# Low parts of projection weights kept in DRAM, with other load orders, in a hybrid decoder layer

## The chip, the cores and the metric

The kernel runs on one core of a Trainium2 chip. The metric is the device time of one execution in microseconds, as the median of several runs. The engines are TensorE (PE, matrix products; its weight loads are shown as PEld), VectorE (DVE), ScalarE (ACT), GpSimd (POOL) and SyncE (SP). SP computes nothing here: it issues loads, in program order (its queue is shown as SPq). POOL issues stores and a few loads.

## The reference

One layer on 2048 tokens of width 1024, in float32. A conditioning vector gives shift, scale and gate vectors (the ada part). The layer is a mixer and an MLP, each behind an RMS norm:

```python
def hybrid_mixer(h, w_in, ..., w_out):
    proj = h @ w_in                       # 1024 -> 4608 and a few columns
    z, xbc, dt_raw, glu_a, glu_b = jnp.split(proj, ...)
    xbc = silu(causal_dwconv(xbc, conv_ssd_w, conv_ssd_b))
    y = ssd_chunked(xh, dt, a, bm, cm) + d_skip * xh
    y = gated_rmsnorm(y, z, ssd_norm_w)
    u = glu_a * sigmoid(glu_b)
    u = causal_dwconv(u, conv_cf_w, conv_cf_b)          # 31 taps
    u = silu(layernorm(u, cf_ln_w, cf_ln_b))
    return concatenate([y, u]) @ w_out    # 2048 -> 1024
# x = x + gate1 * mixer(...);  x = x + gate2 * (relu(h @ w1) ** 2 @ w2);  final RMS norm
```

## The kernel before

**Precision.** Each float32 operand of a large product is split into a high part (a copy rounded to the TensorE format fp32r) and a low part (the rest). A product of two split operands is three matmuls: high by high, high by low, low by high. A weight block is a tile of 128 x 1024 elements, 512 KB. `split_w` loads it on SP, ACT writes the high part and DVE the low part:

```python
raw = t_wr()
nc.sync.dma_start(raw, src)
hi, lo = dst or (t_turn("wh", 2, [P, D], F32R), t_turn("wl", 2, [P, D], F32R))
A.activation(hi, raw, AF.Copy)
V.tensor_tensor(lo, raw, f(hi), SUB)
```

The raw tiles rotate through three buffers (wr0 to wr2), the high and low parts through two each (wh, wl). So the parts of block n+2 can be written only when TensorE has read those of block n.

**Stages.** The tokens are cut into two halves and four quarters of 512 tokens. Times in the profile of before, from the span's start: ada and norm to about 55 us; in_proj, convolutions and SSD of half 0 (36 weight blocks of `w_in`) to about 500, and of half 1 (the same 36 blocks again) to 1009; the mix of half 0, which is out_proj with two quarters of 16 blocks of `w_out` (`mix_q`, L854 to L856), to 1190; up of half 0 to 1500 and its down to 1880; the mix of half 1 (quarters 2 and 3) to 2047; up of half 1 to 2375; its down to 2680; the final norm. Every weight block of `w_in` is thus split twice, and every one of `w_out` four times.

**Up and down.** Up forms its products in a Strassen-like scheme of seven products per block pair (`w1_prep`, products at L1003 to L1005). For each pair mp, DVE makes sums s and u of the weights (L985 to L987, in tiles tp0 and tp1), then ACT and DVE split the seven operands (L885, L886). The raw weights x and y of pair mp+1 come into wr0 to wr2. Down of half 0 is plain (`down_`, L1349 to L1351). Down of half 1 uses seven products too (`down7_of`): the operands that up made (`keep_ops`, stored to DRAM as op_d through POOL) are loaded again (`op_raw`) and split (`op_split`); its weights come through `w2_prep`. `ahead()` is the part of down that is issued beside the last steps of up: it is a generator, and up advances it a step at a time.

**Convolution and layer norm.** `conv_cf` runs at low priority beside other stages and stores its result v_d through POOL. `ln_cf` is the layer norm of that result, for pieces of 256 tokens: load v_d into cu0 and cu1, sum on DVE (L410 to L413), a product with ones on PE (L416, tile bm), squares, a second such product (L213, a part of `chan_rsqrt`), scale, store to m_d (L435). It is a generator; each call of `ln_step` advances it by one step. `ln_step(0)` is called in half 1's in_proj and in the mix of half 0; `ln_step(1)` in half 0's down, one call a weight block.

**What sets the order.** A scheduler of the Tile framework orders instructions by priority within each engine, with the program order as the base; `urgent()` raises a priority, `later()` lowers it. Each engine then runs its own list strictly in order, and so does each issuing queue: an instruction that waits holds up what stands behind it on the same engine.

Of the kernel before, what the change touches and what calls it, by code (L numbers as in the profile page):

```python
# [46 lines left out]
def tile_layer(ctx, tc, x, w_ada, w_mod, vecs, w_in, w_dt, w_out, w1, w2, w2p, out):  # L47
# [243 lines left out]
    def split_w(src, dst=None):  # L291
        raw = t_wr()
        nc.sync.dma_start(raw, src)
        hi, lo = dst or (t_turn("wh", 2, [P, D], F32R), t_turn("wl", 2, [P, D], F32R))
        with urgent():
            A.activation(hi, raw, AF.Copy)  # L296
            V.tensor_tensor(lo, raw, f(hi), SUB)  # L297
        return hi, lo

# [202 lines left out]
    for half in range(2):  # L502
        pre = {}
        if half == 0:
# [5 lines left out]
            for sg in range(4):  # L510
# [3 lines left out]
                held[W0[sg]] = split_w(w_in[W0[sg]], (d_bx(F32R), d_bx(F32R)))  # L514
# [54 lines left out]
            for n, b in enumerate(W1):  # L569
                held[b] = split_w(w_in[b])  # L570
# [9 lines left out]
        else:  # L580
            held = {b: split_w(w_in[b]) for b in W0[:2]}
# [68 lines left out]
        def proj(blk):  # L650
            whl = held[blk] if blk in pre else split_w(w_in[blk])
# [109 lines left out]
        for g in range(2):  # L761
# [44 lines left out]
            whl = split_w(w_in[g * 4 + 1])  # L806
# [9 lines left out]
            whl = [split_w(w_in[g * 4 + 2]), split_w(w_in[g * 4 + 3], (d_bx(F32R), d_bx(F32R)))]  # L816
# [19 lines left out]
    def mix_q(q, acts, x2, side, whl=None):  # L836
# [3 lines left out]
        ws = [w_out[m, pos if q % 2 else 1 - pos] for mg in (0, 4) for pos in range(2) for m in range(mg, mg + 4)]  # L840
        if whl is None:
            whl = split_w(ws[0])
        for mg in (0, 4):
            pss = {}
            for pos in range(2):
                for m in range(mg, mg + 4):
# [15 lines left out]
                    if n < 16:  # L862
                        whl = split_w(ws[n])
# [29 lines left out]
    def mix(half, m0):  # L893
# [25 lines left out]
        def side(n):  # L919
            tick()  # L920
            if half == 0:
                ln_step(0)
# [55 lines left out]
    def w1_prep(sums0):  # L978
        x, y = r2(t_raw(w1[0], "wr0")), r2(t_raw(w1[1], "wr1"))
        for mp in range(NU):  # L980
            src = dict(a11=x[:, 1, :], a22=x[:, 0, :], a12=y[:, 1, :])
            for n in range(2 if mp < NE else 0, 7):
                if n == 2:
                    s, u = (r2(t_at(t)) for t in (("tp0", "tp1") if mp else sums0))
# [89 lines left out]
    def up(half, hx, second, ahead):  # L1074
        early(half, hx, second)
        prep = w1_prep(plan[half][7])
# [147 lines left out]
    def down7_of():  # L1224
# [5 lines left out]

        def op_raw(kb, n):
            return [t_raw(op_d[kb][n][:, h * D : (h + 1) * D]) for h in range(2)]
# [4 lines left out]

        def ahead():
            ws.extend((next(prep), next(prep)))
            yield  # L1240
            raws = op_raw(0, 0)
            yield
            op_split(0, raws)
            ws.append(next(prep))
            raws = op_raw(0, 1)
            yield
            op_split(1, raws)
            raws = op_raw(0, 2)
            ws.append(next(prep))
            yield  # L1250
            op_split(2, raws)
            raws = op_raw(0, 3)
            yield
            op_split(3, raws)
            yield
# [4 lines left out]
        def down():  # L1260
            sqs, ends = [None] * 2, []

            for kb in range(4):
                for g in range(2):
                    b1, b2, b3 = [None] * 2, [None] * 2, [None] * 2
                    raws = None
                    for n in range(7):
                        if kb == 0 and g == 0 and 4 <= n:
                            op_split(n, op_raw(0, n))
# [3 lines left out]
                        for l in range(2):  # L1273
                            mp = 2 * g + l
                            if kb == 0 and n == 0:
# [210 lines left out]
```

## Time and profile before

| | |
|---|---|
| median of 3 runs | 2706.15 us (2704.84 to 2707.09) |
| the profiled execution's own time | 2701.98 us |
| its span | 2699.8 us |
| mean granted TensorE clock | 0.992 |
| PE busy | 2634.3 us, 98% |
| DVE busy | 2181.0 us, 81% |
| ACT busy | 1400.4 us, 52% |
| POOL busy | 300.2 us, 11% |
| moved by DMA | 407.82 MB, mean 151 GB/s |

A row of an engine gives its busy time. A wait is read from the idle time before an instruction and the event that ended it. Where TensorE's granted clock falls to half, a matmul of 512 columns takes 0.43 us from start to start in place of 0.23, and it counts as busy all that time, so idle time and clock are read separately. TensorE's busy time holds ends that are modelled.

### The profile page before, as it was taken

Reading aid. Unit: us, or ns where it says so; the run is one execution under the profiler, and the core shown is the slowest. Engines: PE = TensorE matmul, PEld = TensorE weight load, DVE = VectorE, ACT = ScalarE, POOL = GpSimd, SP = SyncE. Lnnn points to the kernel's source line nnn. Section 1 sums busy time; section 2 is a strip of 40 time slices with the busy share of each in tenths; the row PEclk is TensorE's granted clock in tenths of the full one; section 3 lists DMA queues with packets and bytes.
Section 4 is the critical chain, followed back from the end, with each engine's and each line's share of the span. In section 5 each row is a group of like instructions: output and inputs, shape, how many; then the busy total and the mean of one; then the engine's idle time right before and its main releaser. Section 6 shows DMA issues by size and latency. Waiting matters only on the chain. (4 is left out here: it accounts for less than half of the span.)

```text
span 2699.8 us, 34186 instructions
## 1 busy us (share of the span) xinstructions
PE 2634.3 (98%) x12460; PEld 2149.7 (80%) x12460; DVE 2181.0 (81%) x3368; ACT 1400.4 (52%) x2169; POOL 300.2 (11%) x469
## 2 busy tenths in 40 slices
PE   7999999999999999999999999999999999999997
PEld 4778888788788778888888888878888778778886
DVE  7889999998996668999999874466547776588886
ACT  5757546676754755546566312354336445554452
POOL 1320120030021000011011000000001222100000
PEclk9999999999999999999999999999999999999998
DMA  7463233232322356545434733355735554564541
GB/s 288 140 214 109 79 102 110 86 111 79 118 86 78 123 177 231 164 161 188 148 137 141 242 111 100 109 195 181 244 122 188 204 197 148 197 212 146 167 148 63
DMA packets 130921, 407.82 MB, mean 151 GB/s; under 512 B 15937, under 2 KB 24769, under 8 KB 130753
## 3 DMA queue, kind: packets, MB, share of 16 engines
q1 hardware_dynamic: 97728, 294.07, 32.7%
q0 software_dynamic: 33024, 111.57, 11.6%
q8 instruction: 98, 1.61, 0.2%
q14 instruction: 71, 0.57, 0.1%
HBM read 304.65 MB, written 100.93 MB: 150 GB/s over the span
## 5 line engine op out<-in xcount | busy, mean ns | idle before, releaser
L306 PE MATMUL mm<-big,wh 128*128 128x512 f32 x1024 | 411.3, 402 | 2.4 <-DVE tp L716 1.8
L308 PE MATMUL mm<-big,wl 128*128 128x512 f32 x1024 | 403.9, 394 | 0.0
L307 PE MATMUL mm<-big,wh 128*128 128x512 f32 x1024 | 400.3, 391 | 0.0
L296 ACT ACTIVATE wh<-wr 128x1024 fp32r<-128x1024 f32 x167 | 176.1, 1055 | 314.5 <-PE mm L855 114.0
L297 DVE TENSOR_TENSOR wl<-wr,wh 128x1024 fp32r<-128x1024 f32 x167 | 203.6, 1220 | 70.1 <-ACT wh L296 59.2
L306 PEld LDWEIGHTS mm<-big,wh 128*128 128x128 f32 x1024 | 192.3, 188 | 51.9 <-issue 9.2
L308 PEld LDWEIGHTS mm<-big,wl 128*128 128x128 f32 x1024 | 192.3, 188 | 43.6 <-issue 3.2
L307 PEld LDWEIGHTS mm<-big,wh 128*128 128x128 f32 x1024 | 192.4, 188 | 42.9 <-issue 4.7
L1003 PE MATMUL mm<-big,wh 128*128 128x512 f32 x536 | 212.3, 396 | 9.1 <-ACT wh L885 3.7
L1004 PE MATMUL mm<-big,wh 128*128 128x512 f32 x536 | 210.7, 393 | 0.0
L1005 PE MATMUL mm<-big,wl 128*128 128x512 f32 x532 | 207.2, 389 | 1.2 <-DVE wl L886 1.2
L856 PE MATMUL mm<-big,wl 128*128 128x512 f32 x512 | 200.1, 391 | 1.4 <-DVE wl L297 1.4
L854 PE MATMUL mm<-big,wh 128*128 128x512 f32 x512 | 200.0, 391 | 0.4 <-ACT wh L296 0.4
L855 PE MATMUL mm<-big,wh 128*128 128x512 f32 x512 | 199.3, 389 | 0.0
L1349 PE MATMUL mm<-big,wh 128*128 128x512 f32 x496 | 194.9, 393 | 0.0
L1351 PE MATMUL mm<-big,wl 128*128 128x512 f32 x496 | 194.0, 391 | 0.3 <-DVE wl L297 0.3
L1350 PE MATMUL mm<-big,wh 128*128 128x512 f32 x496 | 194.1, 391 | 0.0
L387 DVE SCALAR_TENSOR_TENSOR ca<-cu,const,ca 128x512 f32<-128x512 f32 x240 | 178.6, 744 | 1.5 <-ACT ca L381 1.2
L390 DVE SCALAR_TENSOR_TENSOR ca<-ca,const,ca 128x512 f32<-128x512 f32 x240 | 178.3, 743 | 0.0
L1005 PE MATMUL mm<-big,wh 128*128 128x512 f32 x440 | 173.3, 394 | 0.0
L1003 PE MATMUL mm<-big,wl 128*128 128x512 f32 x436 | 170.3, 391 | 1.5 <-ACT cc L1113 1.2
L389 DVE SCALAR_TENSOR_TENSOR ca<-cu,const,ca 128x513 f32<-128x513 f32 x224 | 167.2, 746 | 3.7 <-ACT ca L383 3.7
(346 smaller groups left out, 5919.4 us busy)
## 6 DMA issues: line engine op xcount, KB each, us to landing
wr<-in_w_dram SPq DMA_DIRECT2D x120, 512.0 KB, 3.5
wr<-in_w_in_dram SPq DMA_DIRECT2D x72, 512.0 KB, 3.4
wr<-in_w_out_dram SPq DMA_DIRECT2D x64, 512.0 KB, 4.1
wr<-op_d SPq DMA_DIRECT2D x56, 512.0 KB, 4.6
ca<-in_w_ada_dram POOLq DMA_DIRECT2D x64, 256.0 KB, 3.5
tp<-ac_d SPq DMA_DIRECT2D x32, 512.0 KB, 4.3
wr<-m_d SPq DMA_DIRECT2D x32, 512.0 KB, 4.2
op_d<-tt POOLq DMA_DIRECT2D x64, 256.0 KB, 2.6
```

Of the source, the lines that this page charges most:

```text
L297: V.tensor_tensor(lo, raw, f(hi), SUB)
L306: T.matmul(ps, lhsT=hi[:, c], rhs=a[:, 0, :], start=(k == 0), stop=False)
L307: T.matmul(ps, lhsT=hi[:, c], rhs=a[:, 1, :], start=False, stop=False)
L308: T.matmul(ps, lhsT=lo[:, c], rhs=a[:, 0, :], start=False, stop=(k == KT - 1))
L854: T.matmul(ps, lhsT=hi[:, c], rhs=a[:, 0, :], start=(pos + k == 0), stop=False)
L855: T.matmul(ps, lhsT=hi[:, c], rhs=a[:, 1, :], start=False, stop=False)
L856: T.matmul(ps, lhsT=lo[:, c], rhs=a[:, 0, :], start=False, stop=(pos == 1 and k == KT - 1))
L1003: T.matmul(ps, lhsT=hi[:, k], rhs=xs[kp][:, 0, :], start=new and kp == 0, stop=False, skip_group_check=True)
L1004: T.matmul(ps, lhsT=hi[:, k], rhs=xs[kp][:, 1, :], start=False, stop=False, skip_group_check=True)
L1005: T.matmul(ps, lhsT=lo[:, k], rhs=xs[kp][:, 0, :], start=False, stop=kp == KP - 1, skip_group_check=True)
L1349: T.matmul(ps, lhsT=whl[0][:, c], rhs=hi, start=(k == 0), stop=False)
L1350: T.matmul(ps, lhsT=whl[0][:, c], rhs=lo, start=False, stop=False)
```

## The change

First, `split_w` gets a key. At the first use of a block of `w_in` or `w_out` the low part is stored to DRAM (`lo_d`, 52 stores of 512 KB through POOL). At every later use (36 blocks of `w_in`, 48 of `w_out`) SP loads it into the wl tile, and DVE's subtraction is left out: 84 loads of 512 KB, 84 subtractions less. Second, `ln_step` is called in the mix of both halves, and in the last k-block of half 0's down only at every second weight block. Third, in up of half 1 the sums s and u of odd pairs use cu0 and cu1, and not tp0 and tp1. Fourth, down of half 1 uses five raw tiles for its operands (wr0 to wr2, or0, or1), loads each operand a step or more before it is split, spreads the loads of its accumulators, and holds the sum s1 in another tile; `w2_prep` gives up control once more after its first loads. TensorE's instructions stay the same in number. SP has 720 rows in place of 636, POOL 526 in place of 474, DVE 3240 in place of 3340.

```diff
@@ -288,14 +288,26 @@
 
-    def split_w(src, dst=None):
+    lo_d = {}
+    def split_w(src, dst=None, key=None):
         raw = t_wr()
         nc.sync.dma_start(raw, src)
         hi, lo = dst or (t_turn("wh", 2, [P, D], F32R), t_turn("wl", 2, [P, D], F32R))
         with urgent():
             A.activation(hi, raw, AF.Copy)
+            if key in lo_d:
+                nc.sync.dma_start(f(lo), lo_d[key])
+                return hi, lo
             V.tensor_tensor(lo, raw, f(hi), SUB)
+        if key:
+            lo_d[key] = t_dr([P, D], f"lo_d{len(lo_d)}")
+            nc.gpsimd.dma_start(lo_d[key], f(lo))
         return hi, lo
+    def split_in(b, dst=None):
+        return split_w(w_in[b], dst, ("in", b))
 
...
@@ -648,7 +660,7 @@
         def proj(blk):
-            whl = held[blk] if blk in pre else split_w(w_in[blk])
+            whl = held[blk] if blk in pre else split_in(blk)
             r = list(pre.get(blk, []))
...
@@ -837,9 +849,13 @@
         n = 0
-        ws = [w_out[m, pos if q % 2 else 1 - pos] for mg in (0, 4) for pos in range(2) for m in range(mg, mg + 4)]
+        ws = [(m, pos if q % 2 else 1 - pos) for mg in (0, 4) for pos in range(2) for m in range(mg, mg + 4)]
+        def weights(n):
+            return split_w(w_out[ws[n]], key=ws[n])
         if whl is None:
-            whl = split_w(ws[0])
+            whl = weights(0)
         for mg in (0, 4):
...
@@ -860,7 +876,7 @@
                     if n < 16:
-                        whl = split_w(ws[n])
+                        whl = weights(n)
                     side(n - 1)
...
@@ -918,8 +934,7 @@
             tick()
-            if half == 0:
-                ln_step(0)
+            ln_step(half)
             if n in (6, 7, 8, 9, 12, 13, 14, 15):
...
@@ -975,13 +990,14 @@
 
-    def w1_prep(sums0):
+    def w1_prep(half):
+        sums0 = plan[half][7]
         x, y = r2(t_raw(w1[0], "wr0")), r2(t_raw(w1[1], "wr1"))
         for mp in range(NU):
             src = dict(a11=x[:, 1, :], a22=x[:, 0, :], a12=y[:, 1, :])
             for n in range(2 if mp < NE else 0, 7):
                 if n == 2:
-                    s, u = (r2(t_at(t)) for t in (("tp0", "tp1") if mp else sums0))
+                    s, u = (r2(t_at(t)) for t in (sums0 if mp == 0 else ("cu0", "cu1") if half and mp % 2 else ("tp0", "tp1")))
                     V.tensor_tensor(s, y[:, 0:1, :].to_broadcast([P, 2, Q]), x, SUB)
...
@@ -1228,31 +1244,43 @@
 
+        rot = [0]
         def op_raw(kb, n):
-            return [t_raw(op_d[kb][n][:, h * D : (h + 1) * D]) for h in range(2)]
+            rot[0] += 2
+            return [t_raw(op_d[kb][n][:, h * D : (h + 1) * D], ("wr0", "wr1", "wr2", "or0", "or1")[(rot[0] + h) % 5]) for h in range(2)]
 
         def op_split(n, raws):
             for kp in range(KP):
                 ops[n][kp] = split_x(r2(raws[kp // 2])[:, kp % 2, :], ring)
 
+        def acc_load(m):
+            acc[m] = t_at(("tp7", "tp5", "tp4", "tp6", "cu0", "cu1", "state", "ac")[m])
+            nc.sync.dma_start(acc[m], x2_d[1][m])
         def ahead():
+            raws = {0: op_raw(0, 0)}
+            next(prep)
+            yield
+            raws[1] = op_raw(0, 1)
+            yield
+            op_split(0, raws[0])
+            acc_load(0)
+            acc_load(2)
+            yield
+            raws[2] = op_raw(0, 2)
             ws.extend((next(prep), next(prep)))
             yield
-            raws = op_raw(0, 0)
-            yield
-            op_split(0, raws)
+            op_split(1, raws[1])
             ws.append(next(prep))
-            raws = op_raw(0, 1)
-            yield
-            op_split(1, raws)
-            raws = op_raw(0, 2)
+            yield
+            raws[3] = op_raw(0, 3)
+            op_split(2, raws[2])
             ws.append(next(prep))
-            yield
-            op_split(2, raws)
-            raws = op_raw(0, 3)
-            yield
-            op_split(3, raws)
-            yield
+            ready.update(raws)
+            yield
+        ready = {}
 
...
@@ -1265,17 +1293,20 @@
                     for n in range(7):
-                        if kb == 0 and g == 0 and 4 <= n:
-                            op_split(n, op_raw(0, n))
+                        if kb == 0 and g == 0 and 3 <= n:
+                            op_split(n, ready[n])
+                        if kb == 0 and g == 0 and 2 <= n < 6:
+                            ready[n + 1] = ready.get(n + 1) or op_raw(0, n + 1)
+                        if kb == 0 and g == 0 and n == 0:
+                            acc_load(1)
+                            acc_load(3)
+                        if kb == 0 and g == 0 and 2 <= n < 6:
+                            acc_load(n + 2)
                         if g == 1:
                             if kb < 3:
                                 raws = op_raw(kb + 1, n)
                         for l in range(2):
                             mp = 2 * g + l
-                            if kb == 0 and n == 0:
-                                for m in (2 * mp, 2 * mp + 1):
-                                    acc[m] = t_at(f"tp{4 + m}" if m < 4 else ("cu0", "cu1", "state", "ac")[m - 4])
-                                    nc.sync.dma_start(acc[m], x2_d[1][m])
                             if n == 0:
...
@@ -1322,11 +1353,13 @@
                     src[l].update(a21=y[:, 0, :], a12=y[:, 1, :])
+                if kb == 0 and g == 0:
+                    yield
                 for n in range(7):
                     for l in range(2):
                         s = src[l]
                         if n == 2:
-                            s["s1"] = t_turn("tt", 4, [P, Q])
+                            s["s1"] = t_ca()
                             V.tensor_tensor(s["s1"], s["a21"], s["a22"], SUB)
...
@@ -1385,9 +1418,8 @@
                     tick()
-                    if half == 0:
+                    if half == 0 and m % 2:
                         ln_step(1)
-                    if half == 0 and m % 2:
                         nxt += mix_prep(2, len(nxt), plan[1][0])
```

The other places that call `split_w(w_in[...])` call `split_in` in the same way; `up` hands `half` to `w1_prep`.

SP in the mix of quarter 1: weight loads (wr) in the rows of the kernel before.

```order
L293 DMA wr2_1384_9765<-in_w_out_dram 128x1024
L293 DMA wr0_1388_9796<-in_w_out_dram 128x1024
L293 DMA wr1_1392_9827<-in_w_out_dram 128x1024
L293 DMA wr2_1400_9873<-in_w_out_dram 128x1024
L293 DMA wr0_1404_9904<-in_w_out_dram 128x1024
L293 DMA wr1_1409_9943<-in_w_out_dram 128x1024
```

The same place of the changed kernel; wl is the tile of low parts, lo_d the copies in DRAM.

```order
L301 DMA wl0_1386_9872<-lo_d40_9368 128x1024
L296 DMA wr1_1392_9931<-in_w_out_dram 128x1024
L296 DMA wr2_1400_9977<-in_w_out_dram 128x1024
L301 DMA wl1_1390_9903<-lo_d41_9418 128x1024
L296 DMA wr0_1404_10008<-in_w_out_dram 128x1024
L301 DMA wl0_1394_9934<-lo_d42_9454 128x1024
L296 DMA wr1_1409_10047<-in_w_out_dram 128x1024
L301 DMA wl1_1402_9980<-lo_d43_9490 128x1024
L296 DMA wr2_1415_10091<-in_w_out_dram 128x1024
L301 DMA wl0_1406_10011<-lo_d36_9207 128x1024
```

Each load of a low part now stands between the raw loads of later blocks, and must wait on SP until TensorE has read the wl tile.

DVE in up of half 1, about pair 8: L985 to L987 are the sums s and u, L886 a low part, L1103 and L1115 additions for the outputs.

```order
L886 TENSOR_TENSOR wl1_2591_17330<-tp0_2584_17303,wl1_2591_17330 128x512
L987 TENSOR_TENSOR tp1_2585_17304<-wr1_2564_17189,tp1_2585_17304 128x512
L1115 TENSOR_TENSOR cc_2590_17328<-mm2589_17315,up1_2572_17231 128x512
L1103 TENSOR_TENSOR sp1_2592_17345<-mm2582_17288,cc_2590_17328 128x512
L886 TENSOR_TENSOR wh0_2596_17354<-tp0_2584_17303,wh0_2596_17354 128x512
L985 TENSOR_TENSOR tp0_2607_17424<-wr1_2587_17310,wr2_2586_17308 128x1024
L1103 TENSOR_TENSOR sp2_2597_17369<-mm2589_17315,state_2583_17301 128x512
L886 TENSOR_TENSOR wl0_2598_17373<-wr0_2563_17187,wl0_2598_17373 128x512
L1103 TENSOR_TENSOR sp0_2599_17388<-mm2582_17288,up1_2572_17231 128x512
L886 TENSOR_TENSOR wh1_2600_17392<-tp1_2585_17304,wh1_2600_17392 128x512
L986 TENSOR_TENSOR tp1_2608_17425<-wr2_2586_17308,tp0_2607_17424 128x512
```

The same place of the changed kernel, where these lines are L1001 to L1003, L902, L1119 and L1131.

```order
L902 TENSOR_TENSOR wl1_2591_17434<-tp0_2584_17407,wl1_2591_17434 128x512
L1001 TENSOR_TENSOR cu0_2607_17528<-wr1_2587_17414,wr2_2586_17412 128x1024
L1002 TENSOR_TENSOR cu1_2608_17529<-wr2_2586_17412,cu0_2607_17528 128x512
L1119 TENSOR_TENSOR sp1_2592_17449<-mm2582_17392,cc_2590_17432 128x512
L902 TENSOR_TENSOR wh0_2596_17458<-tp0_2584_17407,wh0_2596_17458 128x512
L1003 TENSOR_TENSOR cu1_2608_17529<-wr1_2587_17414,cu1_2608_17529 128x512
L1119 TENSOR_TENSOR sp2_2597_17473<-mm2589_17419,state_2583_17405 128x512
L902 TENSOR_TENSOR wl0_2598_17477<-wr0_2563_17291,wl0_2598_17477 128x512
L1119 TENSOR_TENSOR sp0_2599_17492<-mm2582_17392,up1_2572_17335 128x512
L902 TENSOR_TENSOR wh1_2600_17496<-tp1_2585_17408,wh1_2600_17496 128x512
L1001 TENSOR_TENSOR tp0_2630_17649<-wr1_2610_17535,wr0_2609_17533 128x1024
```

The three operations of one pair's sums stand within five rows; before, the second came five rows behind the first, and the third eight rows behind the second. The sums now change between cu and tp tiles.

SP at the turn into down of half 1: the last loads of up's weights (w1), the operands op_d and the weights w2p.

```order
L974 DMA wr2_2842_18757<-in_w1_dram 128x1024
L974 DMA wr1_2843_18759<-in_w1_dram 128x1024
L974 DMA wr0_2891_19033<-op_d0_0_178 128x1024
L974 DMA wr1_2892_19035<-op_d0_0_178 128x1024
L974 DMA tp0_2884_19005<-in_w2p_dram 128x1024
L974 DMA wr2_2900_19067<-op_d0_1_179 128x1024
L974 DMA tp1_2885_19007<-in_w2p_dram 128x1024
L974 DMA tp2_2886_19009<-in_w2p_dram 128x1024
L974 DMA wr0_2901_19069<-op_d0_1_179 128x1024
L974 DMA tp3_2887_19011<-in_w2p_dram 128x1024
```

In the changed kernel the first half of operand 0 is loaded at the start of up, into or0.

```order
L989 DMA wr0_2495_16981<-in_w1_dram 128x1024
L989 DMA wr1_2496_16983<-in_w1_dram 128x1024
L1100 DMA up0_2503_17000<-p1_d1_0_214 128x512
L989 DMA or0_2885_19111<-op_d0_0_178 128x1024
L989 DMA wr2_2499_16990<-in_w1_dram 128x1024
L989 DMA wr1_2500_16992<-in_w1_dram 128x1024
```

And at the turn itself:

```order
L989 DMA wr2_2842_18861<-in_w1_dram 128x1024
L989 DMA wr1_2843_18863<-in_w1_dram 128x1024
L989 DMA tp0_2886_19113<-in_w2p_dram 128x1024
L989 DMA wr0_2892_19137<-op_d0_1_179 128x1024
L989 DMA tp1_2887_19115<-in_w2p_dram 128x1024
L989 DMA wr1_2902_19186<-op_d0_2_180 128x1024
L1259 DMA cu0_2935_19357<-x2_d1_4_110 128x1024
L989 DMA wr2_2884_19109<-op_d0_0_178 128x1024
```

Operand 1's halves, in or1 and wr0, and the first weights of w2p are asked for before the second half of operand 0, which takes wr2 when up's last weights have left it; the accumulator loads (x2) stand between them.

## Rows read from the trace of the kernel before

**Rows 1.** The page: the span and the busy time of the engines.
```profile
span 2699.8 us, 34186 instructions
...
PE 2634.3 (98%) x12460; PEld 2149.7 (80%) x12460; DVE 2181.0 (81%) x3368; ACT 1400.4 (52%) x2169; POOL 300.2 (11%) x469
```

**Rows 2.** What ended TensorE's idle time, whole span: total, times, longest, us.
```profile
PE bm L416 <- DVE ca L413: 5.0, 1, 5.0
...
PE mm L1003 <- ACT wh L885: 4.0, 3, 2.8
...
PE mm L1003 <- ACT state L1113: 2.3, 1, 2.3
...
PE bm L213 <- DVE ca L427: 1.4, 1, 1.4
...
PE mm L856 <- DVE wl L297: 1.4, 3, 0.5
```

**Rows 3.** The page, costliest groups: the two halves of one weight split.
```profile
L296 ACT ACTIVATE wh<-wr 128x1024 fp32r<-128x1024 f32 x167 | 176.1, 1055 | 314.5 <-PE mm L855 114.0
L297 DVE TENSOR_TENSOR wl<-wr,wh 128x1024 fp32r<-128x1024 f32 x167 | 203.6, 1220 | 70.1 <-ACT wh L296 59.2
```

**Rows 4.** Busy time by windows; last three columns: granted clock, DMA share, GB/s.
```profile
0.00:50.00 50.00, 34.38 (x118) 19.04 (x118) 35.71 (x69) 22.52 (x34) 9.98 (x26) 0.93 0.92 355
1100.00:1150.00 50.00, 49.30 (x225) 40.46 (x224) 48.98 (x75) 26.69 (x37) 5.00 (x8) 1.00 0.47 156
1900.00:1950.00 50.00, 50.00 (x223) 41.40 (x222) 27.05 (x33) 20.26 (x28) 3.04 (x6) 1.00 0.76 250
2150.00:2200.00 50.00, 46.42 (x186) 36.25 (x185) 36.22 (x55) 21.35 (x35) 11.34 (x21) 0.93 0.56 194
2350.00:2400.00 50.00, 44.90 (x182) 35.74 (x181) 38.01 (x62) 25.65 (x46) 5.95 (x11) 0.93 0.75 265
```

**Rows 5.** The chain in the last k-block of the first down stage.
```profile
1805.29 5.62 DMA m_d<-cu
...
1811.30 5.65 DMA cu<-v_d
...
1819.93 1.22 PE bm L416 x2
...
1824.14 0.42 PE mm L1351
1824.56 0.23 PE mm L1349
```

**Rows 6.** The chain in the up stage of the second half.
```profile
2144.80 6.61 DMA wr<-in_w_dram
```

**Rows 7.** Timeline of TensorE behind that load.
```profile
2157.43 0.50 PE L1003 MATMUL mm<-big,tp 128*128 128x512 f32 x1 [1.20 <-ACT tp L885]
...
2159.72 0.80 PE L1003 MATMUL mm<-big,wh 128*128 128x512 f32 x1 [0.71 <-DVE up L1115]
```

**Rows 8.** Timeline at the turn into down: load queue, ScalarE, TensorE.
```profile
2354.47 7.51 SPq L974 DMA_DIRECT2D wr<-op_d  x3
...
2359.28 0.63 ACT L885 ACTIVATE big<-wr 128x512 fp32r<-128x512 f32 x1 [4.10 <-DMA wr<-op_d]
...
2360.44 0.80 PE L1003 MATMUL mm<-big,wh 128*128 128x512 f32 x1 [2.33 <-ACT state L1113]
```

**Rows 9.** The chain at the start of the second down stage.
```profile
2373.23 7.04 DMA op_d<-tt
```

**Rows 10.** Weight loads of out_proj, window 1055:1190: issue to landing.
```profile
DMA to landing us min/median/max: 3.1/3.5/5.5
```

**Rows 11.** The same, window 1850:1950.
```profile
DMA to landing us min/median/max: 3.1/4.5/6.7
```

**Rows 12.** GB/s in 40 slices of 4.125 us, window 1880:2045.
```profile
GB/s 135 125 127 47 348 312 328 336 343 343 277 217 123 209 173 83 282 220 304 198 63 131 127 18 109 129 77 142 166 191 121 70 127 127 106 25 127 231 237 230
```

**Rows 13.** GB/s in 40 slices of 1.25 us, window 0:50.
```profile
GB/s 0 85 339 308 360 338 403 392 397 409 394 419 416 416 406 413 419 393 416 410 410 416 397 413 413 413 420 410 413 400 400 406 413 397 397 416 121 229 190 0
```

More of the change, by code (lines that the diff above doesn't have):

```diff
@@ L513, in tile_layer @@
                     nc.sync.dma_start(wts[sg][j], w_mod[sg, j])
-                held[W0[sg]] = split_w(w_in[W0[sg]], (d_bx(F32R), d_bx(F32R)))
+                held[W0[sg]] = split_in(W0[sg], (d_bx(F32R), d_bx(F32R)))
             x1 = load_x(1)
@@ L569, in tile_layer @@
             for n, b in enumerate(W1):
-                held[b] = split_w(w_in[b])
+                held[b] = split_in(b)
                 pre[b] = [t_mm()]
@@ L580, in tile_layer @@
         else:
-            held = {b: split_w(w_in[b]) for b in W0[:2]}
+            held = {b: split_in(b) for b in W0[:2]}
             hq = [hq0]
@@ L805, in tile_layer @@
             step()
-            whl = split_w(w_in[g * 4 + 1])
+            whl = split_in(g * 4 + 1)
             for qq in range(2):
@@ L814, in tile_layer @@
                     tick()
-            whl = [split_w(w_in[g * 4 + 2]), split_w(w_in[g * 4 + 3], (d_bx(F32R), d_bx(F32R)))]
+            whl = [split_in(g * 4 + 2), split_in(g * 4 + 3, (d_bx(F32R), d_bx(F32R)))]
             for qq in range(2):
@@ L1075, in up @@
         early(half, hx, second)
-        prep = w1_prep(plan[half][7])
+        prep = w1_prep(half)
         ws = [next(prep), next(prep)]
@@ L1236, in op_split @@
                 ops[n][kp] = split_x(r2(raws[kp // 2])[:, kp % 2, :], ring)
+        def acc_load(m):
+            acc[m] = t_at(("tp7", "tp5", "tp4", "tp6", "cu0", "cu1", "state", "ac")[m])
+            nc.sync.dma_start(acc[m], x2_d[1][m])
         def ahead():
+            raws = {0: op_raw(0, 0)}
[8 more added lines that the diff above has]
+            raws[2] = op_raw(0, 2)
             ws.extend((next(prep), next(prep)))
             yield
-            raws = op_raw(0, 0)
-            yield
-            op_split(0, raws)
-            ws.append(next(prep))
-            raws = op_raw(0, 1)
-            yield
-            op_split(1, raws)
-            raws = op_raw(0, 2)
+            op_split(1, raws[1])
             ws.append(next(prep))
             yield
-            op_split(2, raws)
-            raws = op_raw(0, 3)
+            raws[3] = op_raw(0, 3)
+            op_split(2, raws[2])
+            ws.append(next(prep))
+            ready.update(raws)
             yield
-            op_split(3, raws)
-            yield
+        ready = {}
         TO = ((0, 0), (0, 0), (1, 0), (1, 1), (1, 1), (1, 0), (0, 1))
```

## Prediction

> **What bounds the kernel now.** I read the page first. TensorE is busy 2634.3 us of a span of 2699.8 [rows 1]; VectorE follows with 81%. So a saving on VectorE is worth nothing by itself: only what TensorE waits for, and time that it spends at the lower clock, can come back. I then read the list of what ended TensorE's idle time [rows 2], the windows for idle time and clock together [rows 4], and the chain and the timeline at each of the places that they point to [rows 5 to 9]. The columns of the windows are: the window, its length, busy time of PE, PEld, DVE, ACT and POOL, each with a count, then the granted clock, the DMA share and the rate. The reader should see that before's losses inside the work are few and sharp: three places, each a late transfer with a short spell of half clock behind it. Last I read how long a weight load takes to land [rows 10, 11] and how full the DMA already is where more is put in [rows 12, 13].
>
> The profiled execution took 2701.98 us: the span and 2.2 us around it. That is 4.2 us, 0.15%, below the median of the runs, 2706.15. I make the sum against 2701.98 and add the same 4.2 us at the end. TensorE's instructions don't change in number, so the sum has only waits and clock in it.
>
> **The layer norm in the last k-block of the first down.** The store of one piece must land before cu is free (5.62 us), then the next v_d comes in (5.65 us), then DVE sums, then PE's product L416 runs at 1819.93 [rows 5]: 14.6 us from the store. TensorE idles 5.0 us for it and 1.4 us for its like at L213 [rows 2]. Behind the first the clock is at half, 1.2 GHz: matmuls 0.42 us apart until 1824.56, where they are 0.23 apart again [rows 5]. Of 1824.56 - 1819.93 = 4.6 us half is lost, 2.3 us. Sum 5.0 + 1.4 + 2.3 = 8.7 us. A weight block there is 24 matmuls by 0.227 us, 5.45 us, and a step of the norm came with each; load and product are three steps apart, 16.4 us, less the time that the load waited for cu. With a step at every second block they are 32.7 us apart, more than twice the 14.6 us that the chain needs. I take the whole 8.7 us as gained. What was to be done there goes on into the first blocks of the next mix, which has DVE busy 27.05 of 50 us [rows 4]. Bounds: 0 to 8.7.
>
> **Up of half 1.** A load of up's raw weights lands 6.61 us after it was issued [rows 6], and late, because its buffer is released by the third sum (L987), which DVE's order puts thirteen rows behind the first. Behind it TensorE waits in pieces of up to 1.20 us [rows 7]. In the window 2150:2200 it is idle 50 - 46.42 = 3.58 us, and a clock of 0.93 costs (1 - 0.93) x 50 = 3.5 us [rows 4]: together 7.1 us. With the sums of a pair side by side, on tiles of their own, the load starts some eight DVE operations of 0.6 to 0.7 us earlier, about 5 us, against single waits of at most 1.20. I take 6.6, and leave 0.5 to what else meets there. Bounds: 0 to 8.5 (7.1 and the same small waits just ahead of the window).
>
> **The turn into down.** Idle time in 2350:2400 is 50 - 44.90 = 5.10 us, and the clock costs another 3.5 [rows 4], 8.6 together. The first gap: SP waits 7.51 us at three operand loads, ScalarE waits 4.10 us for one of them at 2359.28, and behind it in ScalarE's order stands the copy L1113 that empties the PSUM tile that TensorE's next product wants: TensorE loses 2.33 us [rows 8]. The second: a store of op_d takes 7.04 us to land [rows 9], DVE writes its sum s1 into that tile rotation only after, and TensorE waits 2.8 us for the split, the longest of its line [rows 2]. The change attacks both: three half operands are asked for before up ends, and s1 gets another tile. One edge stays: the second half of operand 0 sits in SP's queue behind an accumulator load into cu0, which has to wait until the last odd pair's u is split, and ScalarE's order still has copies of operand 0 ahead of its L1113. I take 8.1 and leave 0.5. Bounds: 0 to 8.6.
>
> **The subtractions.** 84 by 1.220 us [rows 3] is 102 us of VectorE, all beside TensorE: the only wait for wl in the mix is 1.4 us in all [rows 2]. I count nothing for them, and nothing for that 1.4 either, since the load takes its place. Gains: 8.7 + 6.6 + 8.1 = 23.4 us.
>
> **What the low loads cost.** In the mix a load into wl can be issued only when TensorE ends block n-2, and must land when block n reaches its third matmul: 5.45 + 0.45 = 5.9 us. Landings of the same size were 3.1, 3.5, 5.5 us (least, median, most) in the quieter quarter 1 [rows 10]; there nothing is late, and nothing in quarter 3 or in in_proj, where a block is 48 matmuls, 10.9 us. In quarter 2 they were 3.1, 4.5, 6.7 [rows 11]: there the slowest come 0.8 us late, before any traffic is added. Eight blocks stand in that crowded stretch; eight by 0.8 is 6.4. From the other side: six slices near 335 GB/s [rows 12] are 24.75 us and 8.3 MB; low loads add 512 KB a 5.45 us, 96 GB/s or 2.4 MB. At 343 GB/s, the highest there, 10.7 MB need 31.2 us, 6.4 late; at the 410 GB/s that the start reaches [rows 13], 26.1 us, 1.4 late. Some of it is prefetch that can be late for free. I take 4; bounds 0 to 10 (6.4 and one spell of half clock as at the other places).
>
> The Trainium skill ("DMA: Bandwidth & Descriptors", section "Specifications") gives about 358 GB/s as what HBM feeds one core. By that, as an estimate, the same 10.7 MB would take 29.9 us, 5.1 us late, and the sum would be 1 us worse. The start's slices above 400 GB/s [rows 13] don't agree with it as a limit for this core.
>
> **What the stores cost.** Four fall into the start, where the DMA share is 0.92 over 50 us [rows 4]: 2.1 MB at 410 GB/s are 5.1 us if all are in the way, none if they fall behind the last ada load. I take 1.5. The other 48 go through POOL, which waits there for convolution and norm results. The wl tile must not be rewritten before its store has landed: subtraction 1.2 us and a landing of about 5.6 (the store in [rows 5]) leave 10.9 - 6.8 = 4.1 us for POOL to be late. Where it is later, VectorE's order stalls behind that subtraction, and TensorE two blocks after. VectorE is nearly full in such stretches (48.98 of 50 [rows 4]). Bounds 0 to 6; I take 2.
>
> Sum: -23.4 + 4 + 1.5 + 2 = -15.9. Own time 2686; with the 4.2 us, 2690 at the median.
>
> **The rivals.** *Low loads land late* (slower). Everything speaks for it that makes quarter 2 crowded: each load waits for TensorE at the head of SP's queue, and raw loads, norm loads and accumulator loads queue behind it. It needs a landing plus queueing of 5.9 us to begin. To eat the gain of 19.9 us left after the stores, the sixteen blocks of quarter 2 must be late by 1.25 us each, that is 7.15 us. At 8 us, and half clock for half of that quarter's 87 us, it costs 34 + 22, less 4 already counted: 2690 + 52 = 2742. A milder form, only the eight crowded blocks at 9 us (25) with one spell of clock (3.5), gives 2690 + 24 = 2714. Against it: the rate falls to 123 by the thirteenth slice [rows 12], so half of quarter 2 is free.
>
> *The turn and up keep their gaps.* The residual edge at the turn decides ScalarE's wait again, and up's loads are late for DMA load, not for the sums: only the norm's 8.7 is won, against 7.5 lost: 2705. For it: op_d and weights are loaded at 265 GB/s on average at the turn [rows 4]. Against it: operand 0's first half is asked for a whole stage early.
>
> *All the covers hold.* No loss in quarter 2 or at the stores: 2706 - 23.4 - 1 = 2682 or a little below.
>
> **How the numbers follow.** About 0.2% or 5.4 us is what a measurement can tell from no change. Forecast, 0.55, own range 2683 to 2698; all covers hold, 0.15; gaps stay, 0.15 (half of it within 0.2%, and some of it faster); low loads late, 0.15 (a little of it within 0.2%). So faster 0.75, same 0.11, slower 0.14. Range 2677 to 2711: it reaches into the mild form of late loads, and leaves out the strong one.
>
> **What would show it.** No L416 wait by TensorE, and clock 1.00 through the end of the first down; the raw loads of up landing before DVE asks; ScalarE's wait at 2359 under 1 us; no DVE wait for an op_d store. In quarter 2, waits of L856's successor for DMA into wl of some 4 us in all. The forecast is wrong if these waits come in every block of any quarter, if POOL's stores show up as waits of VectorE's subtraction in half 0, or if the clock falls in a mix.

## The result and the profile after

The changed kernel takes 2735.99 us (2731.97 to 2745.59, 4 runs) against 2705.49 us: ratio 1.012, 95% interval 1.0092 to 1.0148. It is 30 us slower; 2690 was forecast, with 2711 as the end of the range.

The page of the kernel after, and in the second fence its PE waits over the whole span (total, times, longest, us):

```profile
span 2734.1 us, 34341 instructions
PE 2646.6 (97%) x12460; PEld 2159.0 (79%) x12460; DVE 2092.6 (77%) x3284; ACT 1396.8 (51%) x2166; POOL 289.9 (11%) x521
DMA packets 150505, 479.13 MB, mean 175 GB/s; under 512 B 18112, under 2 KB 26944, under 8 KB 150336
L872 PE MATMUL mm<-big,wl 128*128 128x512 f32 x512 | 204.3, 399 | 12.4 <-DMA wl<-lo_d 10.6
```

```profile
PE mm L872 <- DMA wl<-lo_d: 10.6, 7, 3.2
PE sm L213 <- DVE ga L242: 8.2, 3, 3.4
PE bm L428 <- DVE ca L425: 4.2, 1, 4.2
PE mm L870 <- ACT wh L299: 3.4, 1, 3.4
PE mm L318 <- DVE tp L728: 3.2, 1, 3.2
PE mm L1019 <- ACT state L1129: 2.6, 2, 1.7
```

VectorE ran 84 instructions fewer (3284 in place of 3368 in the profiles, one for each subtraction left out) and lost 88 us of work, and 71 MB more are moved. TensorE's waits of [rows 2] are partly gone; others have come or grown. The largest of these, 10.6 us, is for the low parts themselves. But L213, L428, L870 and L318 have no load of a low part in front of them: they wait for DVE and ACT, and all but 2.3 us of L213 (the final norm, as before) lies in in_proj and quarter 1, where the change put in only stores and loads.

Windows of the kernel after (columns as in [rows 4]):

```profile
150.00:200.00 50.00, 44.06 (x245) 35.53 (x245) 40.20 (x68) 26.38 (x50) 14.21 (x27) 0.93 0.72 237
250.00:300.00 50.00, 47.51 (x218) 38.28 (x217) 47.37 (x80) 32.38 (x50) 4.44 (x7) 0.93 0.37 120
1100.00:1150.00 50.00, 45.68 (x193) 36.37 (x192) 44.07 (x65) 19.12 (x24) 7.14 (x12) 0.93 0.84 279
1840.00:1890.00 50.00, 50.00 (x234) 41.68 (x233) 33.49 (x53) 22.50 (x31) 3.03 (x4) 1.00 0.54 180
1940.00:1990.00 50.00, 47.09 (x203) 37.32 (x201) 13.99 (x21) 18.79 (x26) 2.17 (x4) 1.00 0.93 322
2380.00:2430.00 50.00, 47.73 (x208) 38.59 (x207) 39.85 (x64) 32.47 (x59) 7.06 (x13) 1.00 0.83 288
```

Three windows of the kernel before that [rows 4] doesn't have:

```profile
150.00:200.00 50.00, 48.41 (x301) 39.28 (x299) 42.41 (x71) 24.71 (x44) 12.88 (x24) 1.00 0.68 226
250.00:300.00 50.00, 50.00 (x251) 41.24 (x250) 49.04 (x82) 33.06 (x51) 3.08 (x5) 1.00 0.25 85
1800.00:1850.00 50.00, 44.96 (x201) 37.09 (x200) 33.21 (x53) 26.95 (x44) 4.54 (x6) 0.93 0.45 158
```

The end of the first down (1800:1850 before, 1840:1890 now) is without idle time, and at the turn (2380:2430, to be read against 2350:2400 of [rows 4]) the clock stays at 1.00. But the mix that stood at 49.30 busy and a DMA share of 0.47 stands at 45.68 and 0.84. By then the changed kernel is some 30 us behind, so this window holds earlier work; 1125:1175, which holds about the same work, has 45.68 too, at 0.74. Half 0 has more idle time at 150 and 250 than before, and half clock, which was not there.

TensorE runs the same number of matmuls in every kernel, so one can ask how much later the k-th of them starts than in the kernel before, and read off where time goes. The columns are places in the trace of before (us); each profile is one execution, and that of before was some 4 us short of its median, that of stores at first use some 9 us over its own, so read the steps between columns:

| kernel | 522, half 0 projected | 997, half 1 | 1212, both mixes | 1789 | 1841, norm | 1888 | 2054, mixes | 2222, up | 2402, turn | end |
|---|---|---|---|---|---|---|---|---|---|---|
| after | 11.8 | 19.9 | 38.3 | 37.8 | 29.6 | 32.7 | 41.7 | 39.0 | 33.1 | 34.6 |
| no copies | -2.5 | -0.9 | 1.0 | 1.8 | -6.4 | -1.8 | -1.8 | -5.0 | -12.5 | -12.7 |
| copies alone | 16.9 | 25.0 | 46.5 | 45.4 | 44.2 | 45.1 | 56.0 | 55.0 | 56.8 | 56.5 |
| stores at first use | 18.7 | 22.9 | 39.0 | 40.3 | 38.6 | 37.4 | 37.4 | 34.0 | 35.2 | 35.9 |
| small stores | 3.3 | 9.0 | 10.9 | 11.0 | 10.1 | 9.9 | 9.9 | 6.5 | 6.2 | 5.8 |
| small loads | 3.8 | 9.3 | 19.1 | 18.6 | 17.7 | 17.7 | 20.9 | 19.2 | 20.1 | 19.8 |
| loads only | 0.7 | 9.0 | 20.5 | 25.0 | 22.9 | 23.6 | 31.6 | 30.7 | 31.9 | 31.6 |
| norm alone | 5.5 | 8.5 | 8.8 | 8.4 | 1.8 | 3.9 | 3.9 | 5.5 | 5.1 | 5.1 |
| up and turn alone | -1.8 | -2.4 | -0.7 | -0.3 | -2.1 | -2.3 | -2.3 | -8.6 | -15.1 | -14.3 |

After loses 38 us before the first up, in stages where the prediction counted 3.5, wins 8.2 at the norm, gives 3.1 back behind it, loses 9 in the second pair of mixes, wins 2.7 in up (5.1 lost at its start, 7.7 won behind that), and wins 5.9 at the turn.

Two things limit what the table can show. The kernel with the norm's cadence alone runs the same instructions in the same order as the kernel before up to 1778 us, and still has 5.5 and 8.5 in the first two columns: a step of some 5 us there is no more than two executions differ by. And the scheduler sorts each engine's list anew for every kernel. After, no copies, and up and turn alone have another order than before from about 72 us on, in stages that their edits to up and the turn don't touch. At 522 us the two kernels of these without copies stand at -2.5 and -1.8; kernels that still have before's order there and none or two of the full stores (before itself, norm alone, small stores, loads only, small loads) stand between 0 and 5.5.

### The profile page after: what moved, and what is told of

It reads as the page before. It is cut to its first block, busy times and chain, and to the rows that moved or that the text cites. A ratio compares the mean times of both kernels' runs of the same rounds, so it can differ in the third digit from the quotient of the medians.

```text
span 2734.1 us, 34341 instructions
## 1 busy us (share of the span) xinstructions
PE 2646.6 (97%) x12460; PEld 2159.0 (79%) x12460; DVE 2092.6 (77%) x3284; ACT 1396.8 (51%) x2166; POOL 289.9 (11%) x521
## 3 DMA queue, kind: packets, MB, share of 16 engines
q1 hardware_dynamic: 109824, 338.12, 37.8%
## 5 line engine op out<-in xcount | busy, mean ns | idle before, releaser
L318 PE MATMUL mm<-big,wh 128*128 128x512 f32 x1024 | 410.4, 401 | 4.4 <-DVE tp L728 3.2
L320 PE MATMUL mm<-big,wl 128*128 128x512 f32 x1024 | 404.9, 395 | 0.0
L318 PEld LDWEIGHTS mm<-big,wh 128*128 128x128 f32 x1024 | 193.2, 189 | 53.7 <-issue 6.9
L872 PE MATMUL mm<-big,wl 128*128 128x512 f32 x512 | 204.3, 399 | 12.4 <-DMA wl<-lo_d 10.6
L1021 PE MATMUL mm<-big,wl 128*128 128x512 f32 x532 | 207.4, 390 | 2.4 <-DVE wl L902 2.4
L870 PE MATMUL mm<-big,wh 128*128 128x512 f32 x512 | 204.0, 399 | 3.4 <-ACT wh L299 3.4
L1384 PE MATMUL mm<-big,wl 128*128 128x512 f32 x496 | 193.1, 389 | 0.0
L1019 PE MATMUL mm<-big,wl 128*128 128x512 f32 x436 | 169.7, 389 | 0.0
L1020 PE MATMUL mm<-big,wl 128*128 128x512 f32 x436 | 169.6, 389 | 0.0
```

The source lines that it names most:

```text
L318: T.matmul(ps, lhsT=hi[:, c], rhs=a[:, 0, :], start=(k == 0), stop=False)
L320: T.matmul(ps, lhsT=lo[:, c], rhs=a[:, 0, :], start=False, stop=(k == KT - 1))
L870: T.matmul(ps, lhsT=hi[:, c], rhs=a[:, 0, :], start=(pos + k == 0), stop=False)
L872: T.matmul(ps, lhsT=lo[:, c], rhs=a[:, 0, :], start=False, stop=(pos == 1 and k == KT - 1))
L1019: T.matmul(ps, lhsT=hi[:, k], rhs=xs[kp][:, 0, :], start=new and kp == 0, stop=False, skip_group_check=True)
L1020: T.matmul(ps, lhsT=hi[:, k], rhs=xs[kp][:, 1, :], start=False, stop=False, skip_group_check=True)
```

## The experiments

Each was run several times beside the kernel before.

**No copies.** The change without its first part.

```diff
-        if key:
+        if False:
```

> All of the change but its first part: no low part is stored or loaded, every split makes its own. Theory A, the copies in DRAM cause the whole loss: what the changed kernel won at the layer norm (8.2), in up (7.7) and at the turn (5.9) stays, 21.8 us, and nothing else is lost: 2680 to 2690 us against 2705. Theory B, the other parts cost as well (the 5 us lost at the start of up in half 1 are theirs, and their reordering hurts elsewhere): not under 2697.

2690.0 us, ratio 0.9937 (0.992 to 0.9955). Theory A holds within its bounds, at the upper end, though not its "nothing else is lost": by the lag 4.6 us go again behind the norm and 3.5 at the start of up. In two windows of it, the last k-block and the turn, TensorE is idle 0 and 1.12 us at full clock:

```profile
1780.00:1830.00 50.00, 50.00 (x230) 41.58 (x229) 35.77 (x52) 29.91 (x44) 2.26 (x3) 1.00 0.49 153
2340.00:2390.00 50.00, 48.88 (x215) 39.92 (x214) 43.17 (x71) 31.45 (x58) 6.51 (x12) 1.00 0.89 314
```

**Copies alone.** The first part of the change, `split_w` and the places that call it, put into the kernel before.

> The kernel before with the first part alone: stores and loads of the low parts of w_in and w_out. Theory A: the losses that the two traces show up to the first up stage (38 us) and in quarters 2 and 3 (12 us), with none of the gains: 2745 to 2760. Theory B: part of those losses came with the other parts: 2710 to 2735.

2765.44 us, 1.0216 (1.0198 to 1.0235): even above theory A's range. So the first part costs 58 us alone, and the rest wins 17 alone; after stands between them. The two don't add up: 58 less 17 would be 41, and after lost 30. Some 8 of these 11 us lie before the first up (46.5 against 38.3 at 1212), where the two kernels do the same work in another order. That the order is the reason is not shown.

**Copies for one weight.** The same with

```diff
-        if key:
+        if key and key[0] == "in":      # the other: != "in"
```

> The kernel before with copies for w_in only: 36 stores in half 0, 36 loads in half 1, none for w_out. If the stores beside the full DVE and the shifted order of half 0 and 1 cost what the traces differ by until 1000 us: +15 to +20, 2720 to 2726. If w_in's copies are harmless and the loss is a matter of the short blocks of the mix: within 5 us of 2705.

2726.68 us, 1.0064 (1.0046 to 1.0082): 20 us, at the upper end of the first reading.

> The kernel before with copies for w_out only: 16 stores in quarter 0, 48 loads in quarters 1 to 3. If late loads in the mixes cost as the traces show: 12 us in quarters 2 and 3, and some 15 to 20 in quarters 0 and 1: 2730 to 2740. If the loss in quarters 0 and 1 came from w_in's copies, which left the convolution late: 2715 to 2722.

2741.63 us, 1.0127 (1.011 to 1.0143). That is just above the first range. Both kinds cost, 20 and 35 us, and they nearly add up to 58. The loss of quarters 0 and 1 belongs to w_out's own copies: between 997 and 1212 the lag of this kernel grows by 17.0 us, that of the one with w_in's copies by 0.1.

**Stores only, at every use.** The loads are taken out, and the subtraction is made again.

```diff
-            if key in lo_d:
-                nc.sync.dma_start(f(lo), lo_d[key])
-                return hi, lo
```

> The kernel before with the 52 stores of low parts, but never loaded: later uses make their own low part as before. Theory S, the stores hold wl and POOL's queue and with them DVE: the loss of half 0 (some 14 us to 530) and of quarter 0 (5) stays, none in half 1's in_proj or quarters 1 to 3: 2723 to 2732. Theory L, it is the loads: not over 2712.

2765.97 us, 1.021 (1.0182 to 1.0238). The expectation described the kernel wrongly: with these lines out, a store is made at every use, 136 and not 52. So it says nothing on theory S's number. It does show that half 1 now loses time as half 0 does: its lag grows by 22.8 us between 522 and 997, where 36 subtractions and 36 stores stand.

**Stores at the first use only**, as was meant.

```diff
-        if key:
+        if key and key not in lo_d:
```

> The kernel before with the 52 full stores of low parts at the first use and no loads. (The kernel with stores only stored at every use, 136 times.) If a store costs what it did there in half 0 and quarter 0, and what was lost later was the price of the 84 more stores: some 19 us to 530 and 8 to 10 in quarter 0, 2730 to 2738. If the later losses were work put off from half 0: over 2745.

2728.7 us, 1.0085 (1.006 to 1.0109): some 21 us for 52 stores of data that nothing reads. The lag grows until the mixes of half 0 and not after. Just under the range given; the later losses were not work put off from half 0.

**Small stores.**

```diff
-            nc.gpsimd.dma_start(lo_d[key], f(lo))
+            nc.gpsimd.dma_start(lo_d[key][:, :128], f(lo)[:, :128])
```

> The same, but each store moves only 128 of the 1024 columns, 64 KB in place of 512: the same waits on POOL, the same order and the same tile held, an eighth of the traffic. Theory M, the stores' traffic makes the transfers land late on which DVE and ScalarE wait (loads of ac_d 4.4 us before, 5.7 with the stores): the loss goes, 2704 to 2713, and ac_d lands in under 4.7 us. Theory Q, the store's place in POOL's queue and the held tile cost: within 6 us of the full stores.

2706.96 us, 1.0001 (0.999 to 1.0012). The same waits on POOL, and the tile held until its store lands, and no loss: theory M. In this kernel every engine runs before's instructions in before's order, so the place of the stores costs nothing. A small store holds its tile some 2 us less than a full one; but the trace of stores at first use shows no instruction that waited for one of the 52 full ones to land. Until about 1070 us the orders of these two kernels are the same but for a few neighbours changed on VectorE and ScalarE near 355 us, and by 997 us the full stores have lost 14 us more (22.9 and 9.0). So up to there it is the traffic; behind it the order differs too. The DMA issues in the window 60:500 (KB each, median us from issue to landing), of the kernel before, with full stores, with small ones, and after:

```profile
tp<-ac_d SPq DMA_DIRECT2D x16, 512.0 KB, 4.4
u_d<-sp SPq DMA_DIRECT2D x16, 256.0 KB, 3.4
tp<-in_x_dram SPq DMA_DIRECT2D x8, 512.0 KB, 5.1
```

```profile
lo_d<-wl POOLq DMA_DIRECT2D x27, 512.0 KB, 5.7
tp<-ac_d SPq DMA_DIRECT2D x16, 512.0 KB, 5.5
u_d<-sp SPq DMA_DIRECT2D x16, 256.0 KB, 4.6
```

```profile
tp<-ac_d SPq DMA_DIRECT2D x16, 512.0 KB, 4.7
u_d<-sp SPq DMA_DIRECT2D x16, 256.0 KB, 3.8
lo_d<-wl POOLq DMA_DIRECT2D x28, 64.0 KB, 3.7
```

```profile
lo_d<-wl POOLq DMA_DIRECT2D x27, 512.0 KB, 5.2
tp<-ac_d SPq DMA_DIRECT2D x16, 512.0 KB, 5.1
u_d<-sp SPq DMA_DIRECT2D x16, 256.0 KB, 4.8
tp<-in_x_dram SPq DMA_DIRECT2D x8, 512.0 KB, 6.5
```

The broadcast loads ac_d of the SSD land 1.1 us later with full stores. ScalarE waits for them, and VectorE for ScalarE, in the window 60:530 of before, of the full stores and of the small ones:

```profile
DVE tp L696 <- ACT tp L695: 3.2, 3, 1.5
```

```profile
DVE tp L705 <- ACT tp L704: 11.6, 6, 3.6
```

```profile
DVE tp L705 <- ACT tp L704: 5.2, 5, 2.5
```

And TensorE waits for VectorE. With full stores its two longest waits of the window 60:530 are these; all its waits there come to 15.3 us, against 5.8 before and 6.3 with small stores:

```profile
PE sm L221 <- DVE rs L203: 4.5, 1, 4.5
PE sm L719 <- DVE sp L687: 4.2, 1, 4.2
```

Two windows of the kernel before (DVE is the fifth figure) show how little VectorE has to spare there to make up what it idles, 6.3 and 2.5 us of 150:

```profile
200.00:350.00 150.00, 150.00 (x776) 123.81 (x776) 143.74 (x230) 93.22 (x140) 20.00 (x26) 1.00 0.29 96
350.00:500.00 150.00, 148.60 (x838) 120.22 (x836) 147.52 (x236) 78.66 (x125) 14.49 (x12) 1.00 0.35 116
```

In quarter 0, where the other 16 stores stand, the same thing shows on another chain: raw weight, ScalarE's high part, VectorE's low part, TensorE. With full stores (window 1030:1137) and with small ones (the same work, 1015:1110):

```profile
wr<-in_w_out_dram SPq DMA_DIRECT2D x16, 512.0 KB, 5.3
ACT wh L299 <- DMA wr<-in_w_out_dram: 8.1, 4, 3.4
DVE wl L300 <- ACT wh L299: 8.1, 4, 4.9
PE mm L869 <- DVE wl L300: 4.7, 4, 2.3
```

```profile
wr<-in_w_out_dram SPq DMA_DIRECT2D x16, 512.0 KB, 4.6
ACT wh L299 <- DMA wr<-in_w_out_dram: 2.7, 3, 1.4
DVE wl L300 <- ACT wh L299: 3.7, 4, 2.1
```

With small stores TensorE doesn't wait for the low part there at all. The mean DMA share of the stretch is 0.79 with full stores and 0.69 with small ones.

**Loads only.** Two blocks are stored, and every later use loads one of them in place of its own low part.

```diff
-            if key in lo_d:
-                nc.sync.dma_start(f(lo), lo_d[key])
+            if key in seen:
+                nc.sync.dma_start(f(lo), lo_d[key[0] == "in"])
```

> The kernel before with the 84 loads of low parts and only two stores: all loads of w_in read one stored block and all of w_out another, so the low parts are wrong ones and the output too, while the traffic of the loads is the same. Theory L: 2745 to 2760, as with the copies alone (2765). Theory S: the half 0 loss goes, what the loads cost in half 1's in_proj (5 to 9) and in quarters 1 to 3 (20 to 25) stays: 2732 to 2742.

2738.09 us, 1.0112 (1.0092 to 1.0133): theory S's number, 31 us. Stores (21) and loads (31) together make most of the 58. By the lag, 8.3 us of it go in half 1's in_proj, but there norm alone, small stores and stores at first use, which load no low part, show steps of 3.0 to 5.7 as well. 11.5 go from the mixes of half 0 to the start of up behind them (6.3 of these behind 1190), 4.5 in up and down of half 0, where no low part is loaded, and 8.0 in the mixes of half 1.

**Small loads.** The same with an eighth of the bytes; ScalarE fills the rest of the tile.

```diff
-                nc.sync.dma_start(f(lo), lo_d[key[0] == "in"])
+                nc.sync.dma_start(f(lo)[:, :128], lo_d[key[0] == "in"][:, :128])
+                A.activation(lo[:, 128:], raw[:, 128:], AF.Copy)
```

> The kernel with loads only (2738), but each of the 84 loads moves 128 of the 1024 columns, 64 KB in place of 512, and ScalarE fills the other columns with a copy of the raw ones, so the low parts are wrong. The load stands at the same place of SP's order behind the same wait for TensorE. Theory M, the loads' traffic delays others and the loads themselves: the 31 us shrink to 0 to 8, and VectorE's lighter work may even win: 2700 to 2715. Theory Q, the wait at the head of SP's queue holds the raw loads behind it: 2728 to 2740.

2724.0 us, 1.0065 (1.0041 to 1.0088): between the two. Of the loads' 31 us some 13 to 16 are their bytes, by the ratios and by the medians. PE waits with full loads, and with small ones:

```profile
PE mm L874 <- DMA wl<-lo_d: 11.4, 5, 3.0
PE bm L430 <- DVE ca L427: 8.1, 2, 4.8
```

```profile
PE bm L431 <- DVE ca L428: 12.2, 2, 7.4
PE mm L875 <- DMA wl<-lo_d: 2.8, 3, 1.5
```

The waits for the low parts fall from 11.4 to 2.8, and the lag gained in half 1's mixes from 8.0 to 3.2: that part goes with the bytes. What stays lies by the lag at two places. Some 10 us go between 900 and 1050, at the layer norm of half 0 beside half 1's in_proj: 7.4 of the 12.2 us that its product waits for sums on cu fall there (the other 4.8 in the last k-block, as the 5.0 before), and POOL issues the load of cu only when the last piece's store has landed, after 8.2 us of waiting. POOL's and DVE's orders differ from those of the kernel before there. The other 6 go at the start of up of half 0 (1190 to 1212), where loads only loses 6.3 too. Whether the loads' place in SP's queue or the changed order brings this isn't settled; ScalarE's extra copies may have a share.

**Loads from ScalarE's queue.**

```diff
-                nc.sync.dma_start(f(lo), lo_d[key])
+                nc.scalar.dma_start(f(lo), lo_d[key])
```

> The copies alone (2765), but the low parts are loaded from ScalarE's queue in place of SP's. Theory H, the load of a low part stands in SP's order behind raw loads that wait for their own tiles: TensorE's waits for wl by DMA fall from 10.9 us to under 4, and the time to 2745 to 2757. Theory T, the transfers land too late because the DMA is full: the waits stay over 8 us and the time within 6 us of 2765.

2762.99 us, 1.0202 (1.0184 to 1.0219), against 2765.44 for SP's queue: theory T by its numbers. Its first PE waits:

```profile
PE mm L870 <- ACT wh L299: 9.7, 3, 4.7
PE mm L872 <- DMA wl<-lo_d: 8.8, 7, 2.4
```

So SP's queue alone isn't what makes the low parts late, though ScalarE's own order now costs something too.

**The other parts.** The norm's cadence alone (the hunks on `ln_step`), and the tiles in up with the order at the turn alone:

> The kernel before with the layer norm's new cadence alone. If the 4.6 us lost at the start of quarter 2 belong to it: 8 won, 4.6 lost, 2702 to 2705. If they come from the other parts: 2697 to 2700.

2701.64 us, 0.998 (0.9967 to 0.9992): 6 us won, just past the edge of the first reading. By the lag 6.6 come at the norm and 2.1 go again behind it.

> The kernel before with the new tiles for the sums in up and the new load order at the turn into down, without copies and with the old cadence of the norm. Won in up 6.5 and at the turn 7.4, lost 3.5 at the start of up: 2694 to 2698 with the loss at quarter 2's start belonging to the norm; 2698 to 2702 if that loss is here.

2690.49 us, 0.9946 (0.9928 to 0.9965), below the range: without the new cadence the loss at the start of up is small too (1.7). It won 6.3 us in up and 6.5 at the turn by its lag. That leaves some 4 of its 17 us; the order of half 0's in_proj, which it shares with no copies, is the likely place (by the lags at 522 us), but no run separates it.

**No copies, and the norm ended before the mix.** Two steps more in the second quarter of the last k-block:

```diff
-                    if half == 0 and m % 2:
+                    if half == 0 and (m % 2 or qq and m in (2, 6)):
                         ln_step(1)
+                    if half == 0 and m % 2:
```

> The kernel without copies (2690), and two steps of the layer norm more in the second quarter of the last k-block, so that none is left for the mix of half 1. If the 4.6 us that it loses at the start of quarter 2 come from the norm's last product standing there: 2684 to 2687. If the start of quarter 2 is late for its loads alone: within 2 us of 2690.

2691.04 us, 0.9941 (0.9922 to 0.9959): no change. The 4 us lost behind the norm's stage are lost with this cadence too, and not because its last product stands in the mix. In the kernel without copies ScalarE waits 3.37 us there for the first load of w_out; why that load is late with the new cadence wasn't tried.

Of all kernels run, the one without copies (2690.0) and the one with up and turn alone (2690.5) beat both the kernel before and the changed one; the two cannot be told apart: beside the changes to up and the turn, the norm's new cadence won nothing that can be measured.

## Why the prediction was wrong

- **The gains were right in kind, and too large by a quarter.** Counted 23.4; the kernel without copies wins 17. The term that failed is the norm's: 8.7 came as 8.2 at its place (no copies), and 2 to 5 went again behind it, so that alone it is worth 6 (0.2%), and beside the other two parts nothing (17.1 with it, 17.3 without). The step "I take the whole 8.7 us as gained" was too large by that, for a reason that stays open. Up's 6.6 came as 6.3 in up and turn alone, but as 3.2 in no copies, where 3.5 go at the start of the stage; the turn's 8.1 came as 6.5 and 7.5. The edge named there shows as waits for op_d of ScalarE, but in no copies costs TensorE only 1.1 us of idle time. That the sum of 17 comes near the forecast is in part luck, if some 4 us of it are the order of half 0, which the forecast didn't have.
- **The subtractions** were rightly worth nothing.
- **The step that failed most is "What the stores cost".** It priced a store by the tile that it holds and its place on POOL, 2 us, and by bandwidth at the start, 1.5. Holding and place cost nothing (small stores: 0.01%, within 0.12). The 52 stores cost 21 us by what they do to others: in in_proj, at a mean DMA share under 0.5, and in quarter 0, at 0.79, the transfers beside them land 0.4 to 1.6 us later, and where a chain runs load, ScalarE, VectorE, TensorE, and VectorE is 97% busy (in_proj), late landings come through. I had looked only at the two places where the DMA is full, and called the rest free. Of the signs that I named, the clock did fall in a mix; waits of VectorE's subtraction for a store did not come.
- **"What the low loads cost" held where it looked and failed where it put nothing.** In quarter 2 the loads' own waits are 8.8 us: twice the 4 taken, inside the bounds of 0 to 10. From 1900 to 1985 they land at 3.4, 5.5 and 6.8 us (least, median, most), against [rows 11] 3.1, 4.5, 6.7 for the raw loads; all seven waits of TensorE for a low part are for loads that took 5.9 us or more, the mark that was worked out. Quarter 3 has none, as forecast. But quarter 1 has 1.8 us of own waits, and most of the loads' cost comes as waits for others: in loads only some 4 of the 31 us arise in quarter 1, 6 at the start of up behind it, 4.5 in up and down of half 0, and up to 8 in half 1's in_proj, where TensorE waits for VectorE and ScalarE. The sum had no term for these. The rival "low loads land late" had the sign and the sort of price, and was tied to quarter 2 alone. (A slip: 343 GB/s is not the highest rate of [rows 12]; its first full slice has 348, and that bound is then 6.0 us late and not 6.4.)
- **Half clock** multiplies it: in after the windows at 150, 250 and 1100 show 0.93, each some 3.5 us on top of 2 to 6 us idle, as at the places before.

## What to carry to other kernels

Moving work from a full engine into DMA was not free here, even where the mean DMA share was under 0.5: ask which other transfers stand on a chain with no slack, and try the sum with each a microsecond later. Before one accepts such a trade, the test of small transfers (same waits, an eighth of the bytes) can tell traffic from order in one run; look in the trace whether the scheduler has really left the order as it was. A change of several parts is best timed in its parts: here one part cost 58 us alone and hid a gain of 17. And parts need not add up, since each edit can change the order of stages that it doesn't touch.

## What the runs showed of the hardware

- A store of 512 KB from SBUF to DRAM lands in 5.2 to 5.8 us (median, window 60:500) where loads of w_in blocks of that size land in 3.4 to 4.0 (ac_d's broadcast loads in 4.2 to 5.7); a store of 64 KB still needs 3.7.
- With such stores in after, loads and stores beside them in that window land later by 0.4 (w_in, 3.6 to 4.0) to 1.4 us (x, 5.1 to 6.5). The mean share there was far from full: 0.43 and 0.47 in after's windows 200:350 and 350:500, in place of 0.29 and 0.35.
